# A one-core transformer layer on Trainium2: operands of the first half of the tokens made during the last cross sweep, and another order for the first step of the SwiGLU input loop

## The chip, the cores and the metric

The kernel runs on one core of one Trainium2 chip, as a single launch. Its time is the device time of one execution in microseconds (us), and the median over several runs is given. A core has five engines with queues of their own, each worked off in order: TensorE (PE in the rows, its weight loads PEld), VectorE (DVE), ScalarE (ACT), GpSimd (POOL) and SyncE (SP), which here issues all DMAs.

## The reference, cut to what matters

One decoder layer on 1024 tokens with 1024 channels, all in float32:

```python
x = x + 0.5 * swiglu(rmsnorm(x, norm_ffn1), w_ffn1_in, w_ffn1_out)
x = x + hybrid_mixer(rmsnorm(x, norm_mix), w_in, w_out)
x = x + memory_cross_attention(rmsnorm(x, norm_cross), rmsnorm(mem, norm_mem), w_cq, w_ckv, w_co)
x = x + 0.5 * swiglu(rmsnorm(x, norm_ffn2), w_ffn2_in, w_ffn2_out)
return rmsnorm(x, norm_final)

def swiglu(h, w_in, w_out):          # w_in: 1024 x 5632, w_out: 2816 x 1024
    g, u = jnp.split(h @ w_in, 2, axis=-1)
    return (jax.nn.silu(g) * u) @ w_out
```

The two SwiGLU blocks are where the change lies. The memory has 256 tokens, and its keys and values come from `rmsnorm(mem) @ w_ckv`.

## The kernel before, in words

Matrices are multiplied in three passes: each float32 operand is split into a rounded part `hi` (a ScalarE copy) and the rest `lo` (a subtraction on VectorE or GpSimd), and TensorE sums hi·hi, hi·lo and lo·hi.

The input product of a SwiGLU block is done by a scheme of seven block products in place of eight (`ffn_in`, `make_t`). The activations, transposed, are cut into four quarters by channel half j and token half c: `r11`, `r12`, `r21`, `r22` (first index j, second c). `make_t` makes seven operands from them: B11 = r11, B21 = r21, B22 = r22, T1 = r12 - r11, T2 = r22 - T1, T3 = r22 - r12, T4 = r21 - T2, each as hi and lo for two half-quarters h of 256 tokens: per operand two ScalarE copies (L417) and two subtractions (L419), and for the four T operands two more subtractions (L427), written over the quarter they come from. That is 14 copies and 22 subtractions of 128 x 1024.

`ffn_in` then runs 11 steps p, each on 256 gate columns and 256 up columns. A step loads four blocks of weights (512 KB each), makes four combinations `s1` to `s4` of them (`comb`, L497) and seven splits W1 to W7 (hi L215, lo L217), and does seven products of 24 matmuls each (L522), called 1 to 7: product 1 takes B11, 5 T1, 6 T2, 2 B21, 7 T3, 3 B22, 4 T4, in that order. They sum in three PSUM pairs x, y, z: products 1, 6, 7 and 4 all go on in x, and between them x is read into SBUF (`copy` L533 into ta and tb, `add` L536 into td); each waits for the read before it, so product 6 waits for the copy to ta, 7 for the copy to tb, and 4 for the add to td. Silu and four small combinations follow, and the results are stored. The output product `ffn_out` (L630) has no part in the change.

Buffers that bind: ten `hn` buffers (`s_hb`), handed out in the order in which they were asked for, hold the normalized tokens on their way to the transposes, the eight half-quarters, and `sm`, `ta`, `td`, `tb` of a step; four raw buffers take the weight loads; four hi/lo pairs (`s_w`) take the splits.

Where the seven operands lie is decided by memory. `T_EARLY` (B11, T1, T2) lies on the right, which is free from the start of the program, and again when the buffers of the attention and of one half of the activations (`kctx`, `bctx`) are closed; `T_LATE` (B21, T3, B22, T4) lies on the left and needs what was there before to be done. Before the second SwiGLU both are opened by one node, `to_ffn2`, after the whole last sweep.

Ahead of the first SwiGLU runs a loop of eight iterations over the columns of `w_ckv` (L256 to L258, with 256 columns a matmul). Each iteration j also loads token tile j of x, normalizes it (sum of squares on ScalarE L350, two tiny GpSimd instructions L351 and L352, one VectorE instruction L353), transposes it (L300) and copies it into the quarters (L306 and L308). Ahead of the second SwiGLU run four sweeps of the cross attention; a sweep goes twice over the eight token tiles, once for each half of the contraction (`kg`). In the last one each tile is added to the residual in its second pass (L1353), and then spilled, normalized, transposed and copied (`fin_cross`).

The order on every engine is written out ahead by a planner (`Flow.run`): it goes through the nodes like a simulation, takes for each engine the node that can start first by its own cost figures, within 0.15 us the one of lowest `prio`, and for a node that names two engines the one where it would end first, with a `bias` added. `prio` is a stage's base (0, 100, ... 600) plus the order of creation, unless given. The chip then runs each engine's list in that order with real semaphores.

## Time and profile before

| what | us |
|---|---|
| median of 3 runs (lowest, highest) | 2160.08 (2157.78, 2162.36) |
| the profiled execution's own time | 2164.8 |
| its span, first to last instruction | 2163.0 |
| TensorE busy in the span | 2084.8 |
| VectorE busy | 1170.8 |
| ScalarE busy | 808.6 |
| GpSimd busy | 491.5 |

The profile is of one execution. Times in its rows are counted from the start of the span, and "idle before" with a name behind an arrow is what an engine waited for. The busy sums are averages over stages with very different limits, so they say where time is spent and not what a change is worth; that is read in the two stretches around the start of the SwiGLU input loops, at about 69 to 129 us and 1495 to 1561 us.

### The profile page before, as it was taken

To read this page: it belongs to the slowest core of one execution; us is meant where nothing else is said; L and a number is where in the kernel's file an instruction comes from. 1 tells how busy PE (TensorE), PEld (TensorE's weight loads), DVE (VectorE), ACT (ScalarE), POOL (GpSimd) and SP (SyncE) were. 2 spreads that over 40 slices of the span, in tenths; PEclk is the share of its full clock that TensorE was granted. 3 is DMA by queue.
4 is the path that set the end of the run, shared out by engine and by line. 5 is a ranking of instruction groups with operands and counts; after the bars stand their busy time and mean duration, and the time that the engine had idled before them with its cause. 6 is when DMAs were issued, how large, how long until landed. Compare 5 with 4: busy or idle time off the path is not lost.

```text
span 2163.0 us, 25267 instructions
## 1 busy us (share of the span) xinstructions
PE 2084.8 (96%) x9854; PEld 1724.0 (80%) x9854; DVE 1170.8 (54%) x1351; ACT 808.6 (37%) x1138; POOL 491.5 (23%) x341
## 2 busy tenths in 40 slices
PE   7899999999999999998999999998899999999997
PEld 7678888888888788887677788886688888888886
DVE  6956556565447420304896334525855656474464
ACT  5523323234335211114777423304332323333342
POOL 2533342340003100201220001003533233230031
PEclk9999999999999999998999999998999999999999
DMA  8344435457666542226743911112253544558554
GB/s 299 92 161 152 165 132 175 161 205 259 212 194 214 196 115 88 90 106 188 217 120 113 338 40 49 49 49 98 81 185 138 175 159 152 185 187 290 193 196 148
DMA packets 205991, 344.08 MB, mean 159 GB/s; under 512 B 12464, under 2 KB 100656, under 8 KB 205616
## 3 DMA queue, kind: packets, MB, share of 16 engines
q1 hardware_dynamic: 205872, 342.48, 46.9%
q8 instruction: 77, 1.26, 0.2%
q14 instruction: 42, 0.34, 0.0%
HBM read 239.14 MB, written 103.28 MB: 158 GB/s over the span
## 4 chain that ended last, share of the span: by engine, by line
PE 89%; DVE 5%; DMA 2%; issue 1%; ACT 1%; POOL 1%; SPq 0%; POOLq 0%; DVEq 0%; ACTq 0%
PE banks L522 37%; PE banks L630 19%; PE banks L258 9%; PE banks L257 9%; PE banks L256 9%; PE banks L300 2%; PE banks L1113 1%; PE banks L1094 1%; DVE loT L419 1%; DVE loB L419 1%; DMA tqk<-qs 1%; DVE wlo L217 1%; DVE hn L353 1%; PE banks L1057 0%; DVE hn L427 0%
## 5 line engine op out<-in xcount | busy, mean ns | idle before, releaser
L217 DVE TENSOR_TENSOR wlo<-raw,whi 128x1024 fp32r<-128x1024 f32 x159 | 218.2, 1392 | 363.1 <-ACT whi L215 360.0
L215 ACT ACTIVATE whi<-raw 128x1024 fp32r<-128x1024 f32 x168 | 175.2, 1055 | 327.2 <-issue 187.7
L630 PE MATMUL banks<-whi,hH 128*128 128x512 f32 x616 | 240.2, 390 | 0.7 <-DVE hn L648 0.7
L630 PE MATMUL banks<-wlo,hH 128*128 128x512 f32 x616 | 239.7, 389 | 0.0
L630 PE MATMUL banks<-whi,hL 128*128 128x512 f32 x616 | 239.7, 389 | 0.0
L522 PE MATMUL banks<-hiT,whi 128*128 128x512 f32 x704 | 219.6, 394 | 6.2 <-ACT hn L533 6.2
L522 PE MATMUL banks<-loT,whi 128*128 128x512 f32 x704 | 219.1, 393 | 6.5 <-DVE loT L419 6.5
L522 PE MATMUL banks<-hiT,wlo 128*128 128x512 f32 x704 | 218.6, 392 | 0.0
L256 PE MATMUL banks<-whi,aH 128*128 128x512 f32 x512 | 200.9, 392 | 0.0
L258 PE MATMUL banks<-whi,aL 128*128 128x512 f32 x512 | 199.3, 389 | 0.0
L257 PE MATMUL banks<-wlo,aH 128*128 128x512 f32 x512 | 199.3, 389 | 0.0
L536 DVE TENSOR_TENSOR hn<-banks,hn 128x1024 f32<-128x1024 f32 x66 | 80.8, 1224 | 194.2 <-PE banks L522 194.2
L522 PE MATMUL banks<-loB,whi 128*128 128x512 f32 x528 | 165.3, 395 | 7.8 <-DVE loB L419 7.8
L619 DVE TENSOR_TENSOR wlo<-raw,whi 128x1024 fp32r<-128x1024 f32 (+1 forms) x80 | 98.2, 1227 | 126.5 <-ACT whi L617 126.4
L522 PE MATMUL banks<-hiB,whi 128*128 128x512 f32 x528 | 165.0, 394 | 1.6 <-ACT hiB L417 1.6
L617 ACT ACTIVATE whi<-raw 128x1024 fp32r<-128x1024 f32 x84 | 83.1, 989 | 222.3 <-PE banks L630 189.6
L522 PE MATMUL banks<-hiB,wlo 128*128 128x512 f32 x528 | 164.0, 392 | 0.0
L522 PEld LDWEIGHTS banks<-loT,whi 128*128 128x128 f32 x704 | 133.6, 190 | 35.3 <-DVE loT L419 7.3
L522 PEld LDWEIGHTS banks<-hiT,whi 128*128 128x128 f32 x704 | 133.4, 190 | 35.2 <-ACT hn L533 7.5
L522 PEld LDWEIGHTS banks<-hiT,wlo 128*128 128x128 f32 x704 | 133.3, 189 | 28.1
L630 PEld LDWEIGHTS banks<-whi,hH 128*128 128x128 f32 x616 | 115.6, 188 | 25.4 <-issue 1.1
L630 PEld LDWEIGHTS banks<-whi,hL 128*128 128x128 f32 x616 | 115.6, 188 | 24.0
(174 smaller groups left out, 3827.4 us busy)
## 6 DMA issues: line engine op xcount, KB each, us to landing
raw<-in_w_ffn_in_dram SPq DMA_DIRECT2D x88, 512.0 KB, 5.5
raw<-hids SPq DMA_DIRECT2D x70, 512.0 KB, 5.4
hids<-hn SPq DMA_DIRECT2D x66, 512.0 KB, 2.8
hn<-in_w_ffn_out_dram SPq DMA_DIRECT2D x44, 512.0 KB, 4.4
wts<-hn SPq DMA_DIRECT2D x44, 512.0 KB, 2.7
raw<-wts SPq DMA_DIRECT2D x40, 512.0 KB, 3.9
raw<-in_w_ffn_out_dram SPq DMA_DIRECT2D x30, 512.0 KB, 4.0
raw<-in_w_in_dram SPq DMA_DIRECT2D x24, 512.0 KB, 6.2
```

The costliest lines, as they stand in the source:

```text
L215: a = N("ACT", cost_act(1024), lambda: act.activation(hold.v[0], src(), AF.Copy), deps=deps, need=[hold], prio=prio)
L217: lambda e: two[e].tensor_tensor(hold.v[1], src(), f32(hold.v[0]), op=OP.subtract), deps=[a], give=give, prio=prio)
L256: pe.matmul(o, sh, mh, start=start, stop=False)
L257: pe.matmul(o, sh, ml, start=False, stop=False)
L258: pe.matmul(o, sl, mh, start=False, stop=stop)
L300: pe.transpose(need.v[:, k // 4, (k % 4) * P:(k % 4 + 1) * P], src(k), ident)
L419: out.append(N(("DVE", "POOL"), (cost_dve(1024), cost_pool(1024)), lambda e, v=v, ts=ts: two[e].tensor_tensor(TT[name][1][:, :, ts], v(), ...
L522: pe.matmul(b.v[:, f], s_[:, k, f * P:f * P + P], m_[:, k], start=start and k == 0 and n == 0, stop=k == 3 and n == 2, skip_group_check=True)
L536: return N("DVE", cost_dve(S), lambda: dve.tensor_tensor(dst.v, flat(b), dst.v, op=OP.add), deps=deps, give=give)
L617: h = N("ACT", cost_act(n), lambda raw=raw, hold=hold, n=n: act.activation(hold.v[0][:, 0:n], raw.v[:, 0:n], AF.Copy), deps=[ld], need=[hold])
L619: l = N(("DVE", "POOL"), (cost_dve(n), cost_pool(n)), lambda e, raw=raw, hold=hold, n=n: two[e].tensor_tensor(hold.v[1][:, 0:n], raw.v[:, ...
L630: pe.matmul(bs[t // 2].v[:, t % 2], ah.v[s_][:, ts], wh.v[w_][:, ws], start=start and k + q == 0 and i == 0, stop=k + q == NK - 1 and i == ...
```

## The change

- Two more arguments for the planner: `DVE_ONLY` puts a price of 1000 on GpSimd. It holds from the program's start through the first step (p = 0) of the first input loop, and for `make_t` and step 0 of the second; from step 1 on the choice is free as before. The two tiny GpSimd instructions of each norm stay.
- `T_EARLY` is now B11, B21, T1, and `T_LATE` is T2, T3, B22, T4. `make_t` makes them in the order of their use in step 0, with priorities (`TURN`) that put them ahead of the rest of their stage.
- Step 0 has the product order 1, 2, 5, 6, 3, 7, 4 (the others keep 1, 5, 6, 2, 7, 3, 4), loads its weight blocks in the order that this needs, and has priorities of its own for its splits, combinations, copies and adds.
- The last cross sweep takes the two halves of the contraction in the order second, first. After its first pass the right side's former buffers are closed and `T_EARLY` is opened there (`to_early`), in the middle of the sweep.
- In the loop over `w_ckv` the eight token tiles are handled in the first six iterations (`X_AT`).

```diff
--- before.py
+++ after.py
...
 BIAS = {"DVE": 0.75}
+DVE_ONLY = {"POOL": 1000.0}
...
-    T_EARLY, T_LATE = ("B11", "T1", "T2"), ("B21", "T3", "B22", "T4")
+    T_EARLY, T_LATE = ("B11", "B21", "T1"), ("T2", "T3", "B22", "T4")
...
+        TURN = {"B11": -9, "B21": -8, "T1": -7, "T2": -6, "B22": -5, "T3": -4, "T4": -3}
...
+            pr = TURN[name]
...
                 a = N("ACT", cost_act(1024), lambda v=v, ts=ts: act.activation(TT[name][0][:, :, ts], v(), AF.Copy),
-                      deps=deps[h] + [early if name in T_EARLY else late])
+                      deps=deps[h] + [early if name in T_EARLY else late], prio=pr)
                 out.append(N(("DVE", "POOL"), (cost_dve(1024), cost_pool(1024)), lambda e, v=v, ts=ts: two[e].tensor_tensor(
                     TT[name][1][:, :, ts], v(), f32(TT[name][0][:, :, ts]), op=OP.subtract), deps=[a],
-                    give=[src[h]] if give else []))
+                    give=[src[h]] if give else [], prio=pr))
...
-        def minus(dst, a, b, deps):
+        def minus(name, dst, a, b, deps):
             return [[N(("DVE", "POOL"), (cost_dve(1024), cost_pool(1024)), lambda e, h=h: two[e].tensor_tensor(
-                dst[h].v, a[h].v, b[h].v, op=OP.subtract), deps=deps[h])] for h in range(2)]
+                dst[h].v, a[h].v, b[h].v, op=OP.subtract), deps=deps[h], prio=TURN[name])] for h in range(2)]
...
         p1 = parts("B11", r11, has[0])
-        t1 = minus(r11, r12, r11, both(has[0], has[1], each(p1)))
+        p2 = parts("B21", r21, has[0])
+        t1 = minus("T1", r11, r12, r11, both(has[0], has[1], each(p1)))
         p5 = parts("T1", r11, t1)
-        t2 = minus(r11, r22, r11, both(t1, each(p5), has[1]))
+        t2 = minus("T2", r11, r22, r11, both(t1, each(p5), has[1]))
         p6 = parts("T2", r11, t2)
-        p2 = parts("B21", r21, has[0])
-        t3 = minus(r12, r22, r12, both(t1, has[1]))
+        p3 = parts("B22", r22, has[1])
+        t3 = minus("T3", r12, r22, r12, both(t1, has[1]))
         parts("T3", r12, t3, True)
-        parts("B22", r22, both(t2, t3), True)
-        t4 = minus(r11, r21, r11, both(t2, each(p6), each(p2)))
+        t4 = minus("T4", r11, r21, r11, both(t2, each(p6), each(p2)))
         for h in range(2):
-            last[h] = N("X", 0.0, lambda: None, deps=t4[h] + [p2[h]], give=[r21[h]])
+            N("X", 0.0, lambda: None, deps=t2[h] + t3[h] + [p3[h]], give=[r22[h]])
+            N("X", 0.0, lambda: None, deps=t4[h] + [p2[h]], give=[r21[h]])
         parts("T4", r11, t4, True)
...
-            for u, j in ((0, 0), (1, 0), (1, 1), (0, 1)):
+            order = (1, 5, 6, 2, 7, 3, 4) if p else (1, 2, 5, 6, 3, 7, 4)
+            for u, j in ((0, 0), (1, 0), (1, 1), (0, 1)) if p else ((0, 0), (0, 1), (1, 0), (1, 1)):
                 raws[u, j] = load_raw(rows(wi, j * 512, u * DFF + 2 * p * P, 4, 256), 4)
             (a11, l11), (a21, l21), (a22, l22), (a12, l12) = (raws[k] for k in ((0, 0), (1, 0), (1, 1), (0, 1)))
...
+            fl.bias = {} if p else DVE_ONLY
+            turn = {} if p else {i: k - 8.5 for k, i in enumerate(order)}
+            first = None if p else -20
+
+            def comb(i, dst, a, b, op, deps, need=(), give=()):
                 return N(("DVE", "POOL"), (cost_dve(1024), cost_pool(1024)),
-                         lambda e: two[e].tensor_tensor(dst.v, a.v, b.v, op=op), deps=deps, need=need, give=give)
+                         lambda e: two[e].tensor_tensor(dst.v, a.v, b.v, op=op), deps=deps, need=need, give=give, prio=turn.get(i))
             W = {}
...
+            W[1] = split(lambda a11=a11: a11.v, [l11], prio=turn.get(1))
...
+            def split2(a12=a12, l12=l12, W=W, turn=turn):
+                W[2] = split(lambda: a12.v, [l12], prio=turn.get(2))
+            if not p:
+                split2()
+            s1 = comb(5, sm, a21, a22, OP.add, [l21, l22], need=[sm])
+            W[5] = split(lambda sm=sm: sm.v, [s1], prio=turn.get(5))
+            s2 = comb(6, sm, sm, a11, OP.subtract, [W[5][1], l11])
+            W[6] = split(lambda sm=sm: sm.v, [s2], prio=turn.get(6))
+            if p:
+                split2()
+            s3 = comb(7, a21, a11, a21, OP.subtract, [s1, s2, W[1][1]], give=[a11])
+
+            def split7(a21=a21, s3=s3, W=W, turn=turn):
+                W[7] = split(lambda: a21.v, [s3], [a21], prio=turn.get(7))
+            if p:
+                split7()
+            s4 = comb(3, sm, a12, sm, OP.subtract, [W[6][1], W[2][1]], give=[a12])
+            W[3] = split(lambda sm=sm: sm.v, [s4], [sm], prio=turn.get(3))
+            if not p:
+                split7()
+            W[4] = split(lambda a22=a22: a22.v, [l22, s1], [a22], prio=turn.get(4))
...
             def copy(dst, b, deps):
-                return N("ACT", cost_act(S), lambda: act.activation(dst.v, flat(b), AF.Copy), deps=deps, need=[dst])
+                return N("ACT", cost_act(S), lambda: act.activation(dst.v, flat(b), AF.Copy), deps=deps, need=[dst], prio=first)
 
             def add(dst, b, deps, give=()):
-                return N("DVE", cost_dve(S), lambda: dve.tensor_tensor(dst.v, flat(b), dst.v, op=OP.add), deps=deps, give=give)
+                return N("DVE", cost_dve(S), lambda: dve.tensor_tensor(dst.v, flat(b), dst.v, op=OP.add), deps=deps, give=give,
+                         prio=first)
...
             x = Hold(pairs)
...
+            y = z = None
+            for i in order[:-1]:
+                if i == 1:
+                    m1 = prod(1, x, "B11", True)
+                    a = copy(ta, x, [m1])
+                elif i == 5:
+                    z = Hold(pairs)
+                    m5 = prod(5, z, "T1", True)
+                    d = copy(td, z, [m5])
+                elif i == 6:
+                    m6 = prod(6, x, "T2", False, [a])
+                    b_ = copy(tb, x, [m6])
+                elif i == 2:
+                    y = Hold(pairs)
+                    m2 = prod(2, y, "B21", True)
+                    g1 = silu(ta, [add(ta, y, [m2, a], [y])])
+                elif i == 7:
+                    m7 = prod(7, x, "T3", False, [b_])
+                    u2 = add(td, x, [m7, d])
+                else:
+                    m3 = prod(3, z, "B22", False, [d])
+                    g2 = silu(tb, [add(tb, z, [m3, b_], [z])])
...
-    def sweep(ws, evac, korder=(0, 1)):
+    def sweep(ws, evac, korder=(0, 1), middle=None):
...
+            if kg == 0 and middle:
+                middle()
...
+    fl.bias = DVE_ONLY
...
+    X_AT = ((0,), (1, 2), (3,), (4, 5), (6,), (7,), (), ())
     for j in range(8):
         fl.groups = [m_users]
-        x_, xl = ld_rows(x, j)
+        xin = [(i, *ld_rows(x, i)) for i in X_AT[j]]
...
-        hb, sc = norm_scale(lambda x_=x_: x_.v, [xl], g1, None, [x_])
-
...
+        for i, x_, xl in xin:
+            hb, sc = norm_scale(lambda x_=x_: x_.v, [xl], g1, None, [x_])
+
+            def later(i=i, hb=hb, sc=sc):
+                b = Hold(pairs)
+                tr = transposes(lambda k: hb.v[:, k * P:(k + 1) * P], [sc], b, give=[hb])
+                rdone[i] = to_raw(R, tr, b, i)
+            Later.add(1, later)
...
+    fl.bias = {}
...
-    sweep(sweep_w(vos, 512, deps=v_stored), add_x(1, fin_cross))
-    Later.drain()
...
-    fl.base = 600.0
-    fl.groups = []
-
-    def to_ffn2():
-        octx.close()
+    early = []
+
+    def to_early():
         bctx.close()
         kctx.close()
         open_t(ectx, T_EARLY, "right")
+    sweep(sweep_w(vos, 512, (1, 0), v_stored), add_x(1, fin_cross), (1, 0),
+          lambda: early.append(N("SP", 0.0, to_early, deps=t_users + c_users + v_users)))
+    Later.drain()
...
+    fl.base = 600.0
+    fl.bias = DVE_ONLY
+    fl.groups = []
+
+    def to_ffn2():
+        octx.close()
         open_t(lctx, T_LATE, "left")
     sw = N("SP", 0.0, to_ffn2, deps=v_users + t_users + c_users)
-    make_t(R, rdone, sw, sw)
+    make_t(R, rdone, early[0], sw)
     stored = ffn_in(w_ffn2_in, hids2, w_ffn2_out, wts2)
     s_hid.items = None
+    fl.bias = {}
```

## Rows read from the trace of the kernel before

**Rows 1.** The page: busy us by engine (share of the span) and instructions

```profile
PE 2084.8 (96%) x9854; PEld 1724.0 (80%) x9854; DVE 1170.8 (54%) x1351; ACT 808.6 (37%) x1138; POOL 491.5 (23%) x341
```

**Rows 2.** Busy time by stretch: us, engines with instructions, granted clock, DMA share, GB/s

```profile
69.26:128.75 59.49, 46.05 (x178) 36.84 (x177) 46.81 (x27) 26.02 (x28) 29.83 (x13) 0.89 0.26 84
1495.45:1560.96 65.51, 47.48 (x176) 36.93 (x177) 54.73 (x32) 30.02 (x32) 38.96 (x17) 0.84 0.23 81
0.00:69.30 69.30, 58.11 (x456) 57.09 (x456) 49.95 (x48) 37.66 (x53) 19.74 (x28) 1.00 0.80 271
1480.00:1500.00 20.00, 15.45 (x90) 13.07 (x88) 10.39 (x12) 12.33 (x22) 6.04 (x11) 1.00 0.32 131
129.00:167.00 38.00, 38.00 (x169) 31.49 (x168) 22.51 (x18) 12.07 (x12) 12.70 (x8) 1.00 0.45 159
```

**Rows 3.** Waits of TensorE from 1495 to 1561: us in total, times, longest

```profile
PE banks L300 <- DVE hn L353: 4.7, 1, 4.7
PE banks L522 <- DVE loT L419: 4.6, 1, 4.6
PE banks L522 <- DVE loB L419: 3.6, 1, 3.6
PE banks L522 <- ACT hn L533: 3.5, 2, 3.1
PE banks L522 <- ACT hiB L417: 1.6, 1, 1.6
```

**Rows 4.** Timeline of TensorE around the second stretch: start, us, engine, operation, idle before

```profile
1493.54 1.91 PE L300 MATMUL banks<-ident,hn 128*128 128x128 f32 x16
1500.15 1.51 PE L300 MATMUL banks<-ident,hn 128*128 128x128 f32 x8 [4.71 <-DVE hn L353]
...
1508.11 1.22 PE L522 MATMUL banks<-loB,whi 128*128 128x512 f32 x2 [3.60 <-DVE loB L419]
1509.13 1.05 PE L522 MATMUL banks<-hiB,wlo 128*128 128x512 f32 x2
...
1555.52 0.62 PE L522 MATMUL banks<-hiT,whi 128*128 128x512 f32 x2
...
1560.96 0.62 PE L522 MATMUL banks<-hiB,whi 128*128 128x512 f32 x2
```

**Rows 5.** Timeline of TensorE around the first stretch, from the last matmul of the loop

```profile
69.14 0.28 PE L258 MATMUL banks<-mH,wlo 128*128 128x256 f32 x1
...
128.75 0.61 PE L522 MATMUL banks<-hiB,whi 128*128 128x512 f32 x2
```

**Rows 6.** Timelines of VectorE and GpSimd in the second stretch, same columns

```profile
1503.55 1.22 DVE L497 TENSOR_TENSOR raw<-raw,raw 128x1024 f32<-128x1024 f32 x1
1504.68 3.38 DVE L419 TENSOR_TENSOR loB<-hn,hiB 128x1024 fp32r<-128x1024 f32 x1
1508.09 3.28 DVE L427 TENSOR_TENSOR hn<-hn,hn 128x1024 f32<-128x1024 f32 x1
...
1503.71 3.27 POOL L427 TENSOR_TENSOR hn<-hn,hn 128x1024 f32<-128x1024 f32 x1 [4.93 <-DVE loB L419]
1506.94 3.35 POOL L419 TENSOR_TENSOR loB<-hn,hiB 128x1024 fp32r<-128x1024 f32 x1
```

**Rows 7.** Timelines of GpSimd and VectorE: the norm of the last token tile

```profile
1495.53 2.34 POOL L497 TENSOR_TENSOR hn<-raw,raw 128x1024 f32<-128x1024 f32 x1 [2.62 <-PE banks L300]
1497.96 0.19 POOL L351 TENSOR_SCALAR stat_t<-stat_t 128x1 f32<-128x1 f32 x1
...
1498.82 1.28 DVE L353 SCALAR_TENSOR_TENSOR hn<-xt,stat_t,gain 128x1024 f32<-128x1024 f32 x1 [2.48 <-POOL stat_t L352]
```

**Rows 8.** Timeline of GpSimd: a norm instruction while VectorE works on two SBUF operands

```profile
41.12 1.29 POOL L351 TENSOR_SCALAR stat_t<-stat_t 128x1 f32<-128x1 f32 x1
```

**Rows 9.** Timeline of VectorE: the last token's add, and an add behind a product

```profile
1494.15 0.68 DVE L1353 TENSOR_TENSOR xt<-banks,xt 128x512 f32<-128x512 f32 x1
...
1555.72 1.23 DVE L536 TENSOR_TENSOR hn<-banks,hn 128x1024 f32<-128x1024 f32 x1 [4.22 <-PE banks L522]
```

More of the change, by code (lines that the diff above doesn't have):

```diff
@@ L498, in ffn_in @@
             W = {}
-            W[1] = split(lambda a11=a11: a11.v, [l11])
-            s1 = comb(sm, a21, a22, OP.add, [l21, l22], need=[sm])
-            W[5] = split(lambda sm=sm: sm.v, [s1])
-            s2 = comb(sm, sm, a11, OP.subtract, [W[5][1], l11])
-            W[6] = split(lambda sm=sm: sm.v, [s2])
-            W[2] = split(lambda a12=a12: a12.v, [l12])
-            s3 = comb(a21, a11, a21, OP.subtract, [s1, s2, W[1][1]], give=[a11])
-            W[7] = split(lambda a21=a21: a21.v, [s3], [a21])
@@ L553, in ffn_in @@
             x = Hold(pairs)
-            m1 = prod(1, x, "B11", True)
-            a = copy(ta, x, [m1])
-            z = Hold(pairs)
-            m5 = prod(5, z, "T1", True)
-            d = copy(td, z, [m5])
-            m6 = prod(6, x, "T2", False, [a])
-            b_ = copy(tb, x, [m6])
-            y = Hold(pairs)
-            m2 = prod(2, y, "B21", True)
-            g1 = silu(ta, [add(ta, y, [m2, a], [y])])
-            m7 = prod(7, x, "T3", False, [b_])
-            u2 = add(td, x, [m7, d])
-            m3 = prod(3, z, "B22", False, [d])
-            g2 = silu(tb, [add(tb, z, [m3, b_], [z])])
+            y = z = None
[20 more added lines that the diff above has]
+                    g2 = silu(tb, [add(tb, z, [m3, b_], [z])])
             h2 = N(("DVE", "POOL"), (cost_dve(S), cost_pool(S)), lambda e, td=td, tb=tb: two[e].tensor_tensor(
@@ L761 @@
             kvs[j * 256:j * 256 + 256].rearrange("(i p) m -> p i m", p=P), kv.v), deps=[c], give=[kv]))
-        hb, sc = norm_scale(lambda x_=x_: x_.v, [xl], g1, None, [x_])
-        def later(j=j, hb=hb, sc=sc):
-            b = Hold(pairs)
-            tr = transposes(lambda k: hb.v[:, k * P:(k + 1) * P], [sc], b, give=[hb])
-            rdone[j] = to_raw(R, tr, b, j)
-        Later.add(1, later)
+        for i, x_, xl in xin:
[5 more added lines that the diff above has]
+            Later.add(1, later)
         fl.groups = []
```

11 lines of the change are left out of this document (3 added, 8 removed).

## The prediction

> **What bounds the kernel now.** The first look is at the busy times: TensorE works 96% of the span, every other engine about half or less [rows 1]. So only two things can make this kernel faster: less TensorE work, which the change doesn't touch (the same seven products a step, the same matmuls), or less time in which TensorE stands still or runs at its lower clock. The second look, busy time by stretch, finds that time at the start of each SwiGLU input loop: in 69.26 to 128.75 us TensorE is busy 46.05 of 59.49 us at a mean granted clock of 0.89, in 1495.45 to 1560.96 us 47.48 of 65.51 us at 0.84, while from step 1 on it is busy all of 38.00 us at 1.00 [rows 2].
>
> What could be had is read from TensorE's timeline. A product of 24 matmuls takes 1560.96 - 1555.52 = 5.44 us at full clock, seven take 38.08; eight transposes take 0.95 (half of 1.91) [rows 4]. Second stretch: the transposes of the last cross sweep end at 1493.54 + 1.91 = 1495.45; the last token's transposes and seven products could end at 1495.45 + 0.95 + 38.08 = 1534.5. Step 0 ended at 1560.96, so 26.5 us are lost. The waits add up to 4.7 + 4.6 + 3.6 + 3.5 + 1.6 = 18.0 [rows 3]; the other 8.5 are matmuls at the lower level of the clock (0.84 of 2.4 GHz is a mix with 1.2): behind a wait of 3.60 us two matmuls take 1.02 us from start to start (1508.11 to 1509.13) where 0.45 is usual [rows 4]. First stretch: the loop's last matmul ends at 69.14 + 0.28 = 69.42; 69.42 + 0.95 + 38.08 = 108.45, step 0 ended at 128.75, so 20.3 us are lost [rows 5]. Together 46.8 us.
>
> Who ends these waits? Subtractions and copies for the operands, nearly all on VectorE [rows 3]. **Why they are late** is in the timelines of VectorE and GpSimd, side by side. Alone, VectorE starts the next 128 x 1024 subtraction after 1.13 us (1503.55 to 1504.68). As soon as GpSimd has one too (1503.71, 3.27 us), VectorE's takes 3.38 and 3.28, and GpSimd's 3.35 [rows 6]. Two engines do two subtractions in 3.3 us; VectorE alone would do them in 2.3. The help costs 3.3 - 1.13 = 2.2 us on the engine that TensorE waits for, and buys one subtraction of 1.13.
>
> **The change part by part.** *GpSimd priced out.* Step 0 needs 33 such subtractions (22 in `make_t`, 7 splits, 4 combinations), as before; 1.13 us each on VectorE, 37.3 us in all, beside 38.08 us of products. That balance decides everything below.
>
> *Early operands, second stretch.* Six subtractions (B11 and B21, two each, W1, W2) go into the last sweep. There VectorE is busy 10.39 of 20 us and ScalarE 12.33 [rows 2]; 6 x 1.13 = 6.8 us of subtractions fit into 9.6, and as many copies into 7.7 as long as one takes under 1.28, so nothing on the path. What if not: the late ones would follow the sweep, 1.13 each (0 to 6.8; I take 0). After the last token's add ends at 1494.15 + 0.68 = 1494.83 [rows 9] VectorE has 27 subtractions (30.5), the last norm (1.28, rows 7), a token's copies (about 1.3, unless ScalarE takes them) and the adds of products 2 and 3 (2 x 1.13): 35.4, so 1530.2, and I add 2 us for waits on ScalarE's copies between them, an estimate from the one wait on such a copy, 1.6 us [rows 3]; the ends are 0 and 5: 1532.2. TensorE, with no wait, starts product 4 at 1495.45 + 0.95 + 6 x 5.44 = 1529.0. So 3.2 us late. Step 1's combinations and splits may still go to GpSimd, and fall beside this list's end; each costs 2.2 us of VectorE [rows 6]. Between none and four (8.8), I take one: 5.4 us late in all, step 0 ends at 1540, **21.1 us gained**.
>
> *The same, first stretch.* VectorE is busy 49.95 of the 69.3 us before it [rows 2]. With B11, B21, T1 and W1, W2 (ten) done there, 23 subtractions and two adds, 28.3 us, end at 97.7; product 4 is due at 69.42 + 0.95 + 32.64 = 103.0. If none were done early, 33 and two adds would end at 109.0, 6 us late. I take 0 to 6 as bounds and 0.5, nearest the case with the free VectorE time.
>
> *Token tiles earlier in the first loop* (`X_AT`). Two x loads come up to two iterations earlier on SP's queue, ahead of weights, where DMA is at 0.80 and 271 GB/s [rows 2]; 512 KB at that rate are 1.9 us. Two of them late would cost at most 4 us, none if the weights' buffers are what they wait for, and an earlier order could equally gain up to 1 us in the loop; I take 0.5. Eight transposes move from behind the loop into it: the 0.95 above, no change. First stretch: 20.3 - 1.0 = **19.3 gained**.
>
> *Product order and raw loads of step 0.* 1, 2 first gives 2 x 5.44 = 10.9 us of TensorE work which needs only the first half of the tokens and two raw blocks; under it lie the last token's norm and T1. That is the cover of the 4.71 us wait of the last transposes [rows 4]: they now come between products. The cost: product 4 follows 7 directly, and has to wait for the add that reads x. Such an add starts 0.20 us behind the product's end (1555.52 to 1555.72) and takes 1.23 [rows 4, 9]: about 1.6 with the way back. Behind product 4 on TensorE stands step 1. Hidden in the first stretch if step 1's product 1 slips in (its weights are split by then), in the second inside the 5.4; bounds 0 to 3.2 for both, I take 0. Product 3 needs a buffer for td; all ten hold something until a half of r22 is free, 18 VectorE instructions after the norm and copies: 1494.83 + 2.6 + 18 x 1.13 + 2 = 1519.8, due at 1495.45 + 0.95 + 4 x 5.44 = 1518.2. 1.6 late, inside the 5.4 too.
>
> *Turning the sweep's halves, opening the right side in the middle*: the same 192 matmuls and loads; 0, bounds -1 to 1. The spills on SP keep their places. T2 to T4 and B22 still wait for the whole sweep, by which time they are not yet due.
>
> *The norm's two GpSimd instructions stay.* The last token's first one started at 1497.96 because `s1` (2.34 us) lay ahead of it; 1.6 us of that go [rows 7]. But with VectorE busy it takes 1.29 us instead of 0.19 [rows 7, 8], twice: 2.2 more. T1's second half, seventh in the list, is due at 1494.83 + 2.6 + 7 x 1.13 = 1505.3 without this, 1507.5 with it, and product 5 at 1495.45 + 0.95 + 10.88 = 1507.3: covered but for 0.2. The Trainium skill, "SBUF — State Buffer", section "SBUF: two separate sides", calls the port pair of the two engines an exclusive lock, held for a whole instruction by a VectorE operation with two SBUF inputs or by GpSimd, with the loser fully blocked. The 3.38, 3.27 and 1.29 us agree with it. By that rule each such norm loses two VectorE instructions more, and if nothing covered the last one's 2.2 us the sum would be 2122 instead of 2120. The same skill, "Perfetto Trace Analysis", section "Optimizing Scalar/DVE Operations", says that offloading from a saturated VectorE, even to GpSimd, may make sense, but might not help between these two. The 3.3 us for two here are against offloading.
>
> *Later stages.* The planner's lists there start from other clocks; 0, bounds -3 to 3.
>
> **Sum.** 19.3 + 21.1 = 40.4. The profiled execution took 2164.8 us and would take 2124.4; it stands 4.7 above the median of the runs, 2160.08, which would be 2119.7: **2120 us**.
>
> **The rivals.** *Everything fits*: no GpSimd beside the list, all waits hidden: 46.8 gained, 2113. For it: 33 x 1.13 is less than 38.08; against it: the 3.2 worked out above. *VectorE is late in the middle*, product after product: before, 18.0 us of waits drew 8.5 at the lower clock, 0.47 for each. Three waits of 4 us would cost 12 + 5.7 = 17.7, leaving 8.8 in the second stretch and, with half the loss left, 10 in the first: 2160 - 19 = 2141. For it: list and products are of nearly equal length, and td and the add behind product 7 are new places to be late at; against it: the first stretch has 5 us to spare. *The early operands aren't early* (the right side opened late, ScalarE full), which is the change not doing what it says: 6.8 us more on the second list, 2127. *Losses elsewhere eat it*: no change, 2160; it would take 40 us in stages whose code stays, and no row speaks for it. *Slower*: VectorE's 3.3 us are not GpSimd's doing but come with the operands themselves; then one engine has them all. 1494.83 + 30 x 3.3 + 5.44 = 1599 in place of 1561, and 69.4 + 25 x 3.3 + 5.44 = 157 in place of 129: 66 more, 2226. It decides from 1494.83 + 30 c + 5.44 = 1560.96, c = 2.0 us an instruction. For it: the long ones are mostly operand subtractions; against it: the 1.13 between two of them while GpSimd was idle [rows 6].
>
> **How the numbers follow.** 0.61 for the forecast (2115 to 2127), 0.13 for everything fits, 0.13 for late in the middle, 0.06 for not early, 0.03 for no change, 0.04 for slower. Faster by over 0.2% (4.3 us, about what a measurement of this kernel can tell from no change): 0.61 + 0.13 + 0.13 + 0.06 = 0.93; within it 0.03; slower 0.04. The range reaches from everything fits with 3 us from later stages, 2110, to 2138, before the end of late in the middle.
>
> **What would show it.** In the profile after: operand and weight subtractions of step 0 all on VectorE at some 1.2 us; hiB and loB made between 1455 and 1475 (20 us earlier than now), under the sweep; TensorE going from the transposes to product 1 with under 1 us between; step 0 ending near 109 and near 1520 by that profile's own clock; granted clock above 0.95 in both stretches. Wrong would be: VectorE subtractions of 3 us with GpSimd idle, matmul waits of over 3 us for td's copy or for T3, a gap in the loop before 69 us, or step 0 that gains while a later stage loses.

## The result and the profile after

The changed kernel takes **2127.16 us** (median of 4 runs, 2124.55 to 2129.89) where the kernel before takes 2161.22 (4 runs, 2157.78 to 2163.18) on the same chip: ratio 0.9844, 95% interval 0.9826 to 0.9863, 34.1 us less. Forecast were 2120 and a range of 2110 to 2138. The sign and the range held; the gain is 34 where 40 was said. The narrower forecast inside the range, 2115 to 2127, ends just short of it, and 2127 was the number of the rival *not early*; the rows below decide between the two. The profiled execution took 2129.89 us, its span is 2128.1. Lines have moved: transposes are L301, the norm's two GpSimd instructions L352 and L353, its VectorE instruction L354, the subtractions of `make_t` L421 and L429, the combinations L504, the products L541, the read-outs of products L552 and L555.

The page of the changed kernel, busy time by engine (answers to [rows 1]): the work of TensorE is the same, GpSimd does 23 instructions fewer.

```profile
PE 2074.2 (97%) x9854; PEld 1718.0 (81%) x9854; DVE 1149.5 (54%) x1369; ACT 811.9 (38%) x1143; POOL 442.1 (21%) x318
```

Busy time by stretch in the changed kernel (columns as in [rows 2]): step 0 of the first loop, step 0 of the second with the transposes ahead of it, the end of the last sweep, and a long stretch behind the first step 0; then the long stretch in the kernel before.

```profile
73.14:111.25 38.11, 38.11 (x171) 31.54 (x169) 31.56 (x24) 21.51 (x22) 8.96 (x4) 1.00 0.27 90
...
1476.13:1525.97 49.84, 45.04 (x201) 37.17 (x200) 46.35 (x38) 28.45 (x34) 14.26 (x8) 0.93 0.24 83
1455.00:1476.13 21.13, 21.13 (x111) 17.84 (x110) 16.49 (x19) 12.68 (x21) 5.17 (x12) 1.00 0.37 150
111.25:682.50 571.25, 570.51 (x2533) 472.38 (x2532) 328.63 (x283) 203.08 (x215) 158.66 (x86) 1.00 0.55 189
```

```profile
128.75:700.00 571.25, 570.51 (x2533) 472.33 (x2532) 333.41 (x280) 202.92 (x215) 158.49 (x87) 1.00 0.54 187
```

In the first stretch TensorE is now busy all of 38.11 us at full clock, where it was busy 46.05 of 59.49 at 0.89. In the second it is busy 45.04 of 49.84 at 0.93, where it was 47.48 of 65.51 at 0.84 [rows 2]. In the long stretch TensorE is busy 570.51 us in both kernels: the gain is made in these two places.

What is left of the waits (answers to [rows 3]): TensorE's waits from 0 to 120 us, then from 1430 to 1560 us.

```profile
PE banks L301 <- DVE hn L354: 12.4, 5, 8.8
...
```

```profile
PE banks L301 <- DVE hn L354: 3.3, 2, 2.3
PE banks L541 <- DVE hn L555: 1.5, 1, 1.5
```

The 8.8 is the program's start, 8.58 before. No wait on an operand of the two products is left; the waits of transposes for the norm of a token tile stay, and a wait for an add (L555).

The timeline of TensorE around the second stretch (answers to [rows 4]):

```profile
1476.13 1.91 PE L301 MATMUL banks<-ident,hn 128*128 128x128 f32 x16
1480.34 1.84 PE L301 MATMUL banks<-ident,hn 128*128 128x128 f32 x8 [2.30 <-DVE hn L354]
1483.20 1.97 PE L301 MATMUL banks<-ident,hn 128*128 128x128 f32 x8 [1.02 <-DVE hn L354]
1484.82 1.20 PE L541 MATMUL banks<-hiB,whi 128*128 128x512 f32 x2
...
1518.30 0.62 PE L541 MATMUL banks<-hiT,wlo 128*128 128x512 f32 x2
1518.75 0.61 PE L541 MATMUL banks<-hiB,whi 128*128 128x512 f32 x2
...
1521.02 0.61 PE L541 MATMUL banks<-hiB,wlo 128*128 128x512 f32 x2
1523.12 0.73 PE L541 MATMUL banks<-hiT,whi 128*128 128x512 f32 x2 [1.49 <-DVE hn L555]
...
1528.69 0.61 PE L541 MATMUL banks<-hiB,whi 128*128 128x512 f32 x2
```

Product 7 (operand T3) ends with the row at 1518.30. The twelve matmuls from 1518.75 to 1521.02 (operand B11) are half of step 1's product 1, 2.72 us, and run ahead of product 4 (1523.12), so step 0 ends in effect at 1528.69 - 2.72 = 1525.97. Two tiles, two more tiles and seven products could take 1.91 + 1.91 + 38.08 = 41.9; the stretch takes 49.84, so 7.9 us are lost: 2.30 + 1.02 + 1.49 = 4.8 of waits, and 3.1 of matmuls at the clock's lower level behind them (eight transposes take 1.84 and 1.97, where half of sixteen's 1.91 is 0.95; the granted clock is 0.52 from 1480.34 to 1487.45 and 1.00 ahead of it and behind it). Product 1 comes behind the last transposes, not between them.

The same stretch on VectorE and GpSimd (answers to [rows 6, 7]):

```profile
1477.27 1.22 DVE L421 TENSOR_TENSOR loB<-hn,hiB 128x1024 fp32r<-128x1024 f32 x1
...
1479.00 1.28 DVE L354 SCALAR_TENSOR_TENSOR hn<-xt,stat_t,gain 128x1024 f32<-128x1024 f32 x1
...
1485.33 1.22 DVE L421 TENSOR_TENSOR loT<-hn,hiT 128x1024 fp32r<-128x1024 f32 x1
1486.47 1.22 DVE L429 TENSOR_TENSOR hn<-hn,hn 128x1024 f32<-128x1024 f32 x1
...
1514.65 6.14 DVE L421 TENSOR_TENSOR loT<-hn,hiT 128x1024 fp32r<-128x1024 f32 x2
1520.72 1.21 DVE L218 TENSOR_TENSOR wlo<-raw,whi 128x1024 fp32r<-128x1024 f32 x1
1521.85 1.21 DVE L555 TENSOR_TENSOR hn<-banks,hn 128x1024 f32<-128x1024 f32 x1
```

```profile
1477.17 0.55 POOL L353 TENSOR_TENSOR stat_t<-stat_t,mhalf 128x1 f32<-128x1 f32 x1
...
1479.24 2.58 POOL L353 TENSOR_TENSOR stat_t<-stat_t,mhalf 128x1 f32<-128x1 f32 x1
1513.97 2.42 POOL L218 TENSOR_TENSOR wlo<-raw,whi 128x1024 fp32r<-128x1024 f32 x1 [32.14 <-ACT whi L216]
1516.34 3.37 POOL L504 TENSOR_TENSOR hn<-raw,raw 128x1024 f32<-128x1024 f32 x1
```

Subtractions on VectorE start 1.14 us apart (1485.33 to 1486.47) as long as GpSimd has none. When step 1's come to GpSimd at 1514, two on VectorE take 6.14 us in place of 2.35 (the row of a run below). The last of the early operands (`loB` at 1477.27) is made by 1478.5: product 1 had all it needs at least 6.3 us before it started. The wait of 2.30 us is for the norm at 1479.00: its last GpSimd instruction ended at 1477.17 + 0.55 = 1477.72, but on VectorE that `loB` and a copy came first.

### The profile page after: what moved, and what is told of

Its sections match the earlier page's. It is cut to its first block, busy times and chain, and to the rows that moved or that the text cites. A ratio compares the mean times of both kernels' runs of the same rounds, so it can differ in the third digit from the quotient of the medians.

```text
span 2128.1 us, 25253 instructions
## 1 busy us (share of the span) xinstructions
PE 2074.2 (97%) x9854; PEld 1718.0 (81%) x9854; DVE 1149.5 (54%) x1369; ACT 811.9 (38%) x1143; POOL 442.1 (21%) x318
## 4 chain that ended last, share of the span: by engine, by line
PE 91%; DVE 3%; DMA 3%; ACT 1%; POOL 1%; issue 1%; SPq 0%; POOLq 0%; ACTq 0%; DVEq 0%
PE banks L541 39%; PE banks L658 19%; PE banks L259 9%; PE banks L258 9%; PE banks L257 9%; PE banks L301 1%; DMA tqk<-ks 1%; PE banks L1147 1%; PE banks L1128 1%; DMA hn<-kvs 1%; DVE hn L354 1%; PE banks L1091 0%; DVE hn L1096 0%; PE banks L1092 0%; DMA raw<-in_w_ckv_dram 0%
## 5 line engine op out<-in xcount | busy, mean ns | idle before, releaser
L218 DVE TENSOR_TENSOR wlo<-raw,whi 128x1024 fp32r<-128x1024 f32 x162 | 211.1, 1323 | 359.1 <-ACT whi L216 355.6
L541 PE MATMUL banks<-hiT,whi 128*128 128x512 f32 x704 | 216.8, 389 | 1.5 <-DVE hn L555 1.5
L541 PE MATMUL banks<-hiT,wlo 128*128 128x512 f32 x704 | 216.8, 389 | 0.0
L541 PE MATMUL banks<-loT,whi 128*128 128x512 f32 x704 | 216.7, 389 | 0.0
L555 DVE TENSOR_TENSOR hn<-banks,hn 128x1024 f32<-128x1024 f32 x66 | 80.8, 1224 | 191.0 <-PE banks L541 191.0
L541 PE MATMUL banks<-hiB,whi 128*128 128x512 f32 x528 | 163.1, 390 | 0.0
L541 PE MATMUL banks<-loB,whi 128*128 128x512 f32 x528 | 163.0, 390 | 0.0
L541 PE MATMUL banks<-hiB,wlo 128*128 128x512 f32 x528 | 162.9, 390 | 0.0
L541 PEld LDWEIGHTS banks<-hiT,whi 128*128 128x128 f32 x704 | 132.1, 188 | 29.3 <-DVE hn L555 1.9
L541 PEld LDWEIGHTS banks<-hiT,wlo 128*128 128x128 f32 x704 | 132.2, 188 | 27.4
L541 PEld LDWEIGHTS banks<-loT,whi 128*128 128x128 f32 x704 | 132.2, 188 | 27.4
```

The source lines that it names most:

```text
L218: lambda e: two[e].tensor_tensor(hold.v[1], src(), f32(hold.v[0]), op=OP.subtract), deps=[a], give=give, prio=prio)
L541: pe.matmul(b.v[:, f], s_[:, k, f * P:f * P + P], m_[:, k], start=start and k == 0 and n == 0, stop=k == 3 and n == 2, skip_group_check=True)
L555: return N("DVE", cost_dve(S), lambda: dve.tensor_tensor(dst.v, flat(b), dst.v, op=OP.add), deps=deps, give=give, prio=first)
```

## The experiments

Each number is a median in us, beside the kernel before measured on the same chip. The changed kernel itself was measured twice, 2127.16 and, beside the last group, 2125.83 (5 runs, 2123.33 to 2130.5); single runs of it differ by up to 7 us, and differences below 2 are read from the stretches alone. Up to the last group a difference to the changed kernel is taken from 2127.16, which was measured apart from these runs: the kernel before took 2161.22 beside it and up to 2162.64 beside them. Against 2125.83 a loss would be 1.3 us larger and a gain 1.3 us smaller. Each kernel has its own line numbers; operations and operands tell which line is which.

**The price alone.** GpSimd's price is put into the kernel before, at the places where the change has it; everything else stays.

```diff
+DVE_ONLY = {"POOL": 1000.0}
...
+            fl.bias = {} if p else DVE_ONLY
...
```

> The kernel before with nothing but GpSimd priced out in the same places. If the company of GpSimd is what made the operands late (theory), most of the gain is here: VectorE's subtractions all at 1.2 us, step 0 of the second stretch ends near 1494.8 + 33 x 1.13 + 3.8 + 2 + 5.4 = 1543 in the clock of the kernel before (was 1561) and that of the first near 113 (was 129): about 2130. If early operands and the product order are what counts (rival), less than a third of the 34 us: 2150 or more.

Measured: 2151.09 (before 2162.64), ratio 0.9952 [0.9937, 0.9967], 11.5 less. The theory was wrong by 21 us; the rival's number came, but the next run shows that it wasn't for the rival's reason. Rows of that kernel, TensorE's and VectorE's timeline, show why:

```profile
1516.83 1.22 PE L524 MATMUL banks<-hiT,wlo 128*128 128x512 f32 x2 [10.14 <-DVE wlo L218]
```

```profile
1505.34 3.48 DVE L428 TENSOR_TENSOR hn<-hn,hn 128x1024 f32<-128x1024 f32 x3
...
1515.56 1.21 DVE L218 TENSOR_TENSOR wlo<-hn,whi 128x1024 fp32r<-128x1024 f32 x1
```

Each subtraction takes the 1.2 us hoped for, but the split of W6 stands behind nearly all of `make_t`, since the list goes by order of creation; TensorE waits 10.14 us for it. A fast list in the wrong order keeps 11.5 us of the 30 that the next run has.

**The price with the order of the list.** The same, with `TURN`, `turn` and `first`, in the product order of before.

```diff
+        TURN = {"B11": -9, "T1": -8, "T2": -7, "B21": -6, "T3": -5, "B22": -4, "T4": -3}
...
+            turn = {} if p else {i: k - 8.5 for k, i in enumerate((1, 5, 6, 2, 7, 3, 4))}
...
```

> The kernel before with GpSimd priced out and, beside that, priorities for make_t and step 0 in the order in which its own (old) product order uses them; nothing is opened or loaded earlier. With the price alone TensorE waited 10.1 and 4.4 us for W6's lo, which stands behind nearly all of make_t on VectorE. Theory: price and order of the list belong together; with both these waits go to under 2 us and the time to 2132 to 2138. Rival: without early operands VectorE's list is too long whatever its order, and the waits only change their name: 2146 or more.

Measured: 2132.49 (before 2162.48), 0.9863 [0.9848, 0.9878]: 30.0 less, as the theory said. The two together are most of the change; all the rest of it adds 4 us. Step 0 of the first loop ends at 108.32 here, 2.9 us ahead of the changed kernel's 111.25 and as early as the prediction thought possible (108.45). TensorE's timeline there, then the longest waits from 1440 to 1560 us:

```profile
108.32 0.62 PE L529 MATMUL banks<-hiB,whi 128*128 128x512 f32 x2
```

```profile
PE banks L301 <- DVE hn L354: 4.1, 1, 4.1
PE banks L529 <- DVE wlo L218: 2.1, 1, 2.1
PE banks L529 <- ACT hiB L420: 1.6, 1, 1.6
...
```

The first and third stand ahead of product 1 and are what the rest of the change is about. The 2.1 stands in step 1 (at 1536.99; in the first loop one of 1.59 at 121.86).

**Everything but the price.** In the changed kernel.

```diff
-DVE_ONLY = {"POOL": 1000.0}
+DVE_ONLY = {}
```

> The changed kernel with GpSimd free to take subtractions everywhere. Theory: the planner gives it about a third of them again, VectorE's take 3.3 us beside them, and each stretch gets 8 to 12 us longer: 2145 to 2150. Rival: early operands cover that, under 5 us in all: below 2133.

Measured: 2142.22, 0.9916 [0.9897, 0.9935]; 15.1 above the changed kernel. It lies nearest the theory, 3 us below its range. So early operands, order and turns (the priorities) are worth 20 without the price, and the price 15 on top; alone it was worth 11.5.

**The right side opened late.** `to_early` moved behind the whole last sweep, the sweep's halves in their old order.

```diff
-    sweep(sweep_w(vos, 512, (1, 0), v_stored), add_x(1, fin_cross), (1, 0),
-          lambda: early.append(N("SP", 0.0, to_early, deps=t_users + c_users + v_users)))
+    sweep(sweep_w(vos, 512, deps=v_stored), add_x(1, fin_cross))
...
+        to_early()
         open_t(lctx, T_LATE, "left")
...
-    make_t(R, rdone, early[0], sw)
+    make_t(R, rdone, sw, sw)
```

> The changed kernel with the early operands of the second SwiGLU opened only after the whole last sweep, which takes its halves in the old order. Theory: TensorE's list has the last two tokens' transposes ahead of product 1 anyway, until about 1484.8, so four subtractions more on the list behind the sweep cost 3 to 5 us, 2130 to 2132. Rival (product 1 and 2 under the sweep's end are the point): 10 us or more, 2137. First stretch unchanged to 0.5 us.

Measured: 2131.07, 0.986 [0.9844, 0.9877]: 3.9 more, as expected. Only four of the six early subtractions are late here, those of B11 and B21, 4 x 1.13 = 4.5 us on VectorE; W1 and W2 are still split under the sweep. The four cost 3.9 us. Its longest waits of TensorE in the second stretch:

```profile
PE banks L541 <- DVE loB L421: 2.3, 1, 2.3
PE banks L541 <- DVE hn L555: 2.2, 1, 2.2
...
```

**The old product order.** Step 0 in the order 1, 5, 6, 2, 7, 3, 4; the turns of its splits and combinations follow, those of `make_t` stay.

```diff
-            order = (1, 5, 6, 2, 7, 3, 4) if p else (1, 2, 5, 6, 3, 7, 4)
+            order = (1, 5, 6, 2, 7, 3, 4)
```

> The changed kernel with the old product order (1, 5, 6, 2, 7, 3, 4) in step 0, its weights' turns and loads alone as changed. Theory: product 5 needs T1 right behind product 1, which VectorE can give with a wait of about 1 us, and product 6 needs T2 and W6, 3 us late: +3 to +5 us in the second stretch, 0 to 1 in the first, 2130 to 2133; the wait for the add ahead of product 4 (1.5 us) goes. Rival: the product order is what makes early operands worth anything: +8 us or more, 2135.

Measured: 2130.19, 0.9854 [0.9839, 0.9869]: 3.0 more, in the theory's range, but not by its mechanism. TensorE's timeline in the second stretch:

```profile
1525.29 0.62 PE L541 MATMUL banks<-hiB,whi 128*128 128x512 f32 x2
...
1538.60 0.73 PE L541 MATMUL banks<-hiT,wlo 128*128 128x512 f32 x2 [1.37 <-DVE wlo L218]
```

In step 0 there is no wait for T1, T2 or W6, and the wait for the add ahead of product 4 is gone. Step 0 ends at 1525.29, 47.84 us behind the sweep's end (1477.45), where the changed kernel takes 49.84; in the first stretch it ends at 111.30, as in the changed kernel. Two waits for a weight split come back, but in step 1: 1.59 at 124.84 and 1.37 at 1538.60. So no run shows that the new order gains anything within step 0. By the end of step 1 this profile is 2.0 us behind the changed kernel's in the first stretch and 0.3 ahead in the second; where the rest of the 3.0 lies stays open.

**One token tile per iteration** in the loop over `w_ckv`, as before the change.

```diff
-    X_AT = ((0,), (1, 2), (3,), (4, 5), (6,), (7,), (), ())
+    X_AT = ((0,), (1,), (2,), (3,), (4,), (5,), (6,), (7,))
```

> The changed kernel with one token tile in each of the eight turns of the first loop, as before. Theory: the three waits of TensorE on norms in the loop (2.7 us) go, the last tile's norm comes after the loop and costs at most its 1 us of transposes, since products 1 and 2 need only the first half: step 0 of the first stretch ends at 108.5 to 111 instead of 111.25, so -3 to 0 us. Rival (the earlier tiles are needed for T1): a wait of 3 us or more for T1 or for the transposes behind the loop, so 1 to 5 us slower than the changed kernel.

Measured: 2125.25, 0.983 [0.9815, 0.9844]: 1.9 less. The waits that go are visible. First the longest of them in the changed kernel, on TensorE and with the GpSimd instruction behind it, then what is left of TensorE's waits from 0 to 135 us in this run:

```profile
54.06 1.09 PE L301 MATMUL banks<-ident,hn 128*128 128x128 f32 x8 [1.60 <-DVE hn L354]
```

```profile
50.56 1.49 POOL L352 TENSOR_SCALAR stat_t<-stat_t 128x1 f32<-128x1 f32 x1 [8.96 <-ACT hn L351]
```

```profile
PE banks L301 <- DVE hn L354: 9.9, 2, 8.7
...
```

With two norms in one iteration the second is late: 12.4 us of waits in five places became 9.9 in two, both near the program's start. TensorE's timeline in this run shows the end of step 0:

```profile
109.91 0.62 PE L541 MATMUL banks<-hiB,whi 128*128 128x512 f32 x2
```

Product 1 starts at 68.97 in place of 73.14, and step 0 ends in effect at 109.91 - 2.72 = 107.19, 4.1 us earlier than in the changed kernel's first profile and 3.4 earlier than in its second (110.56).

**The price in step 1 too.**

```diff
-            fl.bias = {} if p else DVE_ONLY
+            fl.bias = {} if p > 1 else DVE_ONLY
```

> The changed kernel with GpSimd priced out in step 1 too. Theory: the two T4 subtractions that took 6.1 us beside GpSimd take 2.3, so the wait of 1.5 us ahead of product 4 in the second stretch goes; the rest is hidden: 1.5 us less, 2125.5. Rival: with step 1 all on VectorE its list grows into step 1's products and a new wait of 2 us or more appears there: 2127 or more.

Measured: 2141.75, 0.991 [0.9894, 0.9926]: 14.6 more; the rival was right, and by more than it said. TensorE's and VectorE's timeline of this run, then GpSimd's in the changed kernel:

```profile
121.42 1.22 PE L541 MATMUL banks<-hiT,whi 128*128 128x512 f32 x2 [5.59 <-ACT whi L216]
...
1526.34 0.62 PE L541 MATMUL banks<-hiT,whi 128*128 128x512 f32 x2
```

```profile
113.15 1.22 DVE L600 TENSOR_TENSOR hn<-hn,banks 128x1024 f32<-128x1024 f32 x1 [4.88 <-PE banks L541]
...
118.99 1.22 DVE L504 TENSOR_TENSOR hn<-raw,raw 128x1024 f32<-128x1024 f32 x1
...
1519.52 2.35 DVE L421 TENSOR_TENSOR loT<-hn,hiT 128x1024 fp32r<-128x1024 f32 x2
```

```profile
96.73 3.04 POOL L504 TENSOR_TENSOR hn<-raw,raw 128x1024 f32<-128x1024 f32 x1 [37.77 <-DMA raw<-in_w_ffn_in_dram]
```

On VectorE step 1's first combination `s1` (L504) stands behind an instruction that waits 4.88 us for product 4, and starts at 118.99. GpSimd has nothing of that kind in its list and makes it at 96.73, slowly, but 22 us earlier. Here GpSimd is worth its 3.04 us as a second list. Both stretches have this wait of 5.59 us and one of 1.59 behind it, 14.4 us together. What the theory named did come as well: T4's two subtractions take 2.35 us in place of 6.14, and product 4 (1526.34) starts without a wait.

**A higher cost of the norm told to the planner** (1.3 and 1.6 us for the two GpSimd instructions of tiles 5 to 7, 0.2 and 0.5 so far; in the changed kernel's profile the first ones take 0.91, 0.19 and 0.19 us, the second ones 0.55, 0.55 and 2.58, so the told cost fits none of the three).

```diff
...
-        hb, sc = norm_scale(lambda: X(t), [xlast[t]], g4[0])
+        hb, sc = norm_scale(lambda: X(t), [xlast[t]], g4[0], st=(1.3, 1.6) if t > 4 else (0.2, 0.5))
```

> The changed kernel with the planner told that the two tiny GpSimd instructions of the last three tokens' norms of the last sweep take 1.3 and 1.6 us (0.2 and 0.5 before), as they do beside a busy VectorE. It then puts product work ahead of the last transposes on TensorE. Theory: of the 8.1 us lost in the second stretch the two waits on norms (3.3 us) and the lower clock behind them (about 3 us) go: 4 to 6 us less, 2121 to 2123. Rival: VectorE's list is the limit and what is saved there comes back as a wait for T1 or T2: within 1.5 us of the changed kernel.

Measured: 2125.58, 0.9834 [0.9816, 0.9852]: 1.6 less, nearer to the rival and not to be told from nothing. Its TensorE still goes through all transposes first, with waits of 0.65, 1.54 and 2.66 us between them:

```profile
1476.88 1.09 PE L301 MATMUL banks<-ident,hn 128*128 128x128 f32 x8 [1.54 <-DVE hn L354]
1480.63 1.24 PE L301 MATMUL banks<-ident,hn 128*128 128x128 f32 x8 [2.66 <-DVE hn L354]
1481.52 1.20 PE L541 MATMUL banks<-hiB,whi 128*128 128x512 f32 x2
```

So a higher figure for the norm doesn't bring product 1 ahead. The PSUM pairs are handed out in the order in which they are asked for (`Hold(pairs)`), and the last transposes ask before product 1 does. The next run tests that.

**Product 1's pair asked for ahead.**

```diff
         def later():
+            if t == 6:
+                ahead.append(Hold(pairs))
             b = Hold(pairs)
...
-            x = Hold(pairs)
+            x = ahead.pop(0) if ahead else Hold(pairs)
```

> The changed kernel with one edit: the PSUM pair of product 1 (x) is asked for just ahead of the transposes of token tile 6 of the last cross sweep, so that the queue of pairs, which serves in order of asking, lets product 1 start between the last transposes. Nothing else differs. Theory (product 1 stood behind the last two tiles' transposes because of its place in that queue, though its operands were made by 1478.5 us): the waits of 2.3 and 1.0 us on the norm before product 1 go, and the slow clock behind them; product 1 starts near 1478 instead of 1484.8; 2.5 to 6 us less than the changed kernel, 2121 to 2124.5. Rival (VectorE's list is the bound by now, and the place of product 1 only decides where TensorE waits): the wait comes back in front of product 4 or 5, 3 to 5 us longer there, and the time is within 1.5 us of the changed kernel's.

Measured: 2126.32 (before 2161.96), 0.9835 [0.9822, 0.9849], against 2125.83 for the changed kernel beside it: nothing in the whole. Its timeline of TensorE (products are L543 here, the add L557):

```profile
1473.54 1.91 PE L301 MATMUL banks<-ident,hn 128*128 128x128 f32 x16
1475.21 0.71 PE L543 MATMUL banks<-hiB,whi 128*128 128x512 f32 x2
...
1478.03 1.03 PE L301 MATMUL banks<-ident,hn 128*128 128x128 f32 x8
...
1481.64 1.03 PE L301 MATMUL banks<-ident,hn 128*128 128x128 f32 x8
...
1490.83 0.97 PE L543 MATMUL banks<-loT,whi 128*128 128x512 f32 x2 [2.25 <-DVE loT L421]
...
1518.52 0.72 PE L543 MATMUL banks<-hiT,whi 128*128 128x512 f32 x2 [1.79 <-DVE hn L557]
```

The cause is shown: with its pair, product 1 starts as soon as the sweep's last transposes are through, the next eight come between its halves, the last eight behind it, and the two waits are gone. The price named for them was too high. From the sweep's last pair of transposes to the first matmul of product 4 it is 1518.52 - 1473.54 = 44.98 us, where the changed kernel has 1523.12 - 1476.13 = 46.99 and, measured again, 47.07: 2.0 us less. The rest came back as the rival had it, as 2.25 us at the start of product 5, since VectorE has T1's rest (L421) no sooner, with matmuls at the lower level behind it (granted clock 0.72 from 1490 to 1496), and 0.3 more in front of product 4. In the two profiles the whole doesn't show the 2.0, because the sweep ended 1.7 us later than in the changed kernel's beside it (1471.88), in stages that are the same in both; that the medians differ for this reason too isn't shown.

**Pair and tiles together, and both with the norm's higher cost.** The edits are those above.

> The pair asked for ahead (as in the run before) and one token tile per iteration in the loop over w_ckv. Theory: the two gains lie in different stretches and add up: 1.9 us (the tile per iteration alone) on top of the pair's gain, 2119 to 2122.5. Rival: they do not add, because the lists behind them are planned anew: within 1 us of the better of the two, 2123 to 2125.

> As the run before, and the planner told that the norm's two GpSimd instructions of tiles 5 to 7 take 1.3 and 1.6 us. Theory: with the pair ahead product 1 covers the last norms anyway, so the price adds nothing: within 1 us of the run before. Rival: the right price still moves the last norms and with them T1, 1.5 us less, as it did alone.

> The changed kernel again, unedited, beside the others on the same chip: 2125.5 to 2129 by the first measurement. It is the base from which the gains of the other runs of this call are taken.

Measured: 2121.2 (4 runs, 2117.14 to 2121.95; 0.9806 [0.9793, 0.982]) for two edits, 2120.26 (4 runs, 2119.48 to 2120.76; 0.9805 [0.9792, 0.9819]) for three, 2125.83 for the changed kernel again (0.9833 [0.9819, 0.9846]). No run of the three-edit version is as slow as any of the changed kernel's, and it is the best here: 5.6 us under it. The gains of the two stretches add up as read there: 4.6 by the medians, where the stretches have 2.0 and between 2.5 (12.4 - 9.9 of waits) and 4.1. By the medians of the runs alone, 1.9 and nothing, it would not have been seen. The norm's price adds 0.9, within the spread, as the theory said. In the three-edit version the second stretch has waits of TensorE of 2.0, 1.0, 0.7 and 0.4 us, the longest again in front of T1's rest:

```profile
1487.23 0.74 PE L543 MATMUL banks<-loT,whi 128*128 128x512 f32 x2 [2.00 <-DVE loT L421]
```

The norm's two small instructions on VectorE were not tried.

## Why the prediction was right, and where it was off

*What bounds the kernel, and why the operands are late.* Right, and shown by the runs with the price alone, with price and order, and without the price. All of the gain is in the two stretches, and VectorE's 3.3 us were GpSimd's doing: without it every subtraction takes 1.22. The rival *slower* fell with that (1485.33 to 1486.47).

*First stretch.* Forecast 19.3; step 0 ends in effect at 111.25 (half of step 1's product 1 is ahead of product 4 here too), 128.75 - 111.25 = 17.5. The products have no wait left, as said. The term that was mis-sized is `X_AT`: 0.5 was taken, with bounds of -1 and 4, and product 1 starts at 73.14 where 69.42 + 0.95 = 70.4 was possible: 2.8. It was looked for in the loads; it came from two norms in one iteration, as the run with one tile per iteration shows (product 1 at 68.97). So the tiles handled earlier cost this stretch 3.4 to 4.1 us.

*Second stretch.* Forecast 5.4 us lost, measured 7.9, so 26.5 - 7.9 = 18.6 gained in place of 21.1. The step that failed is "That is the cover of the 4.71 us wait of the last transposes [rows 4]: they now come between products". They come ahead of them, and the wait isn't covered: it became two, 2.30 and 1.02; the pair asked for ahead shows that the queue of PSUM pairs is why. Whoever follows an order written out ahead has to look at every queue that a step stands in, and buffers handed out in order of asking are one. With the cover given, 2.0 us are gained, and VectorE's list binds instead, at T1: the balance of 37.3 us of subtractions and 38.08 of products, which the prediction named, leaves little to gain beyond. The other half of that step, the order 1, 2 ahead of 5, gains nothing in step 0 by any run: with the old order it was 2.0 us shorter.

*Early operands.* Three of the four `loB` subtractions start under the sweep, the last at 1477.27, just behind its end at 1476.13; TensorE is busy all of 21.13 us ahead of that end. So the operands were early, and the rival *not early* is out, though 2127 was its number. The cost of 0 was too low by about 1.2 us: the last `loB` and a copy delay a norm from 1477.72 to 1479.00, and the wait for that norm is 2.30 where the run opened late has 1.10. Six subtractions were counted as moved; W1 was split under the sweep in the kernel before too (1467.24). The four of B11 and B21 are worth 3.9.

*Product 4 behind product 7, and GpSimd beside the end of the list.* The wait was put at about 1.6 and is 1.49, but that the numbers agree is luck. The 1.6 is an add that starts 0.20 us behind product 7; half of step 1's product 1 slipped in, and its 2.72 us cover that. The add came 2.9 us late: product 7 ends at 1518.30 + 0.62 = 1518.92, the add starts at 1521.85, behind T4's subtractions and a split on VectorE. One GpSimd instruction of 2.2 was taken there; two came (1513.97 and 1516.34) and cost VectorE 6.14 - 2.35 = 3.8. With GpSimd priced out in step 1 too they are gone, and the wait with them. So the 1.49 is GpSimd's doing. The 3.2 us by which the list alone was to be late didn't show, for TensorE had lost 7.9 - 1.49 = 6.4 us ahead of it.

*The norm's GpSimd instructions.* The last tile's second one takes 2.58 us where the one before takes 0.55: 2.0 more, against 2.2. It was said to be covered, and wasn't: the wait of 1.02 us is for the norm behind it. The exclusive port pair that the Trainium skill describes ("SBUF — State Buffer", section "SBUF: two separate sides") fits the 2.58, the 1.49 and the 6.14; the case that the prediction worked out by that rule, with nothing to cover the last norm's 2.2, is the one that came. The other page of the Trainium skill that the prediction cites, "Perfetto Trace Analysis", section "Optimizing Scalar/DVE Operations", holds that moving work off a saturated VectorE may make sense even to GpSimd, but might not help between these two. Both of its halves are in this kernel: it doesn't help in step 0 (15.1 us), and does in step 1 (14.6).

*Later stages.* Forecast 0. The two stretches give 17.5 + 18.6 = 36.1, the spans differ by 2163.0 - 2128.1 = 34.9; the 1.2 between are no more than the stages ahead of the sweep's end vary from one profile of the same kernel to another (1476.13 and 1471.88).

*From profile to median.* The span gained 34.9 where 40.4 was said. Another 2.0 us of the 7 between 2120 and 2127.16 come from the step to the median: the profile before stood 4.7 above it, the one after stands 2.7 above.

*The signs named beforehand.* Subtractions at 1.2 us (but for T4's), no idle time between transposes and product 1, and a granted clock of 1.00 in the first stretch came as said. Missed were 1455 to 1475 for hiB and loB (to 1478.5), the ends near 109 and 1520 (111.25 and 1525.97) and the clock of the second stretch (0.93, not above 0.95). One sign of being wrong came: gaps in the loop before 69 us (the longest 1.60).

## What to carry to other kernels

Price a second engine by what it does to the first: here one GpSimd instruction cost VectorE 2.2 us, so pricing it out paid where VectorE's list was due, and lost as much one step on, where GpSimd ran ahead of a VectorE that was waiting. Which of the two it is can change within a step: at the end of step 0 the same help still cost a wait of 1.49 us. Making the list faster without putting it in the order of need kept little over a third of the gain (11.5 of 30). Where work is planned ahead, a step can't pass what asked earlier for the same buffers, and covering one wait is worth only the distance to the next: 3.3 us of waits taken away, and 3.1 of matmuls at the lower clock with them, gave 2.0.

## What was not expected

An instruction of GpSimd on 128 x 1 elements takes 0.55 us or 2.58 (1477.17 and 1479.24), by what VectorE does beside it; a planner that has it at 0.5 is wrong by 2 us. After the wait of 2.30 us eight transposes take TensorE 1.84 us, after the one of 1.60 in the first loop 1.09. The granted clock of the stretch is 0.93, a mix of the levels 2.4 and 1.2 GHz, and the 3.1 us lost at the lower level are 0.65 of the waits' 4.8, where before the change it was 0.47 [rows 3, 4]. That share is no constant of a wait: the loss lies behind the two waits for norms, while behind the 1.49 the clock is granted in full (1.00 from 1523.12 to 1528.69), and in the run opened late it stays at 1.00 from 1475.9 to 1485 across waits of 1.10, 1.13, 0.51 and 2.27 us. What decides it, no run here shows.
